# Row factors of the second norm taken in the output projection, and the second block's first rows turned during the first block's last up projection

## Chip, cores and metric

The kernel runs on one core of a Trainium2 chip. The metric is the device time in microseconds of one execution. Before the change the median of three runs is 1966.64 us (1966.62, 1966.64 and 1971.97).

## The reference, cut to what matters

Two independent sequences, a prompt of 512 rows and a sample of 1024 rows, each 1024 wide, go through one layer and a last norm. The change lies between the mixer and the SwiGLU.

```
def rmsnorm(x, g):
    y = x * rsqrt(mean(x * x, axis=-1) + EPS)
    return y * g

def trunk(x, ...):
    x = x + hybrid_mixer(rmsnorm(x, norm1_g), ..., w_out)   # mixed @ w_out
    x = x + swiglu(rmsnorm(x, norm2_g), w_gate, w_up, w_down)
    return rmsnorm(x, final_norm_g)

def swiglu(hn, w_gate, w_up, w_down):
    return (silu(hn @ w_gate) * (hn @ w_up)) @ w_down
```

## The kernel before

The 1536 rows are twelve tiles of 128 rows: a0 to a3 of the prompt, b0 to b7 of the sample. Until about 746 us the kernel computes the first norm, the mixer's projections, attention and the linear attention. Then comes the output projection: for each tile of the sample, class `Out` loads the mixed rows transposed (`mr`), splits them into a high and a low part (`mh`, `ml`), multiplies them with `w_out` in three column pieces (`acco` in PSUM), adds each piece to the residual row tile `xr` on VectorE (DVE), and `store` writes the finished tile to the DRAM tensor `x2d`.

The SwiGLU works on two blocks of six tiles: block 0 is a0 to a3, b0, b1; block 1 is b2 to b7. Each block goes through eleven groups of inner columns. A group has seven gate products and seven up products (a Strassen-like scheme over the operands b11, t2, b21, t3, t1, t4, b22, each as a high and a low part, into `gu` banks) and then six `down` steps, one for each row tile, of twelve matmuls each (two column halves of six, into `dn` banks, each half added to the accumulator `xa` on DVE). Weights are loaded by DMA (`rw_gate`, `rw_up`), combined on DVE with temporaries from the pool `sm`, and split into `cw_gate`, `cw_up` by ScalarE (ACT) and DVE.

The operands of a block are made by two methods. `rows(i)` loads row tile i of the block from `x2d` into `hx` (a pool of two buffers), squares it on ACT with a row sum (written to a `junk` tile of `sm`), makes the row factor (`ms` on DVE, a power on GpSimd), and scales `hx` by it and by the norm's weight on DVE. `turn(q)` takes row tiles 2q and 2q+1, transposes them on TensorE (PE) in four quarters of four 128x128 blocks (`trf`, sixteen in all), and makes the seven operands of these columns from them: copies and high parts on ACT, sums and low parts on DVE, with two temporaries `xt` from `sm`, which also has two buffers. So a block needs three turns, and the `hx` buffers of a turn are free for the next pair of rows when its transposes are done. For block 0 the turns stand in the output projection, between the tiles b2, b3 and b4, with two PSUM banks `tr`; for block 1 they stand at the boundary, in the last group of block 0, with the four `dn` banks.

The order of the program's lines is not the order on the engines: a scheduler orders the instructions of each engine, every engine runs its own in that order, and the DMAs named here are issued from one queue, SP's. At the boundary `rows(0)` and `rows(1)` of block 1 are written after up products 2 and 4 of the last group, and a turn after downs 0, 2 and 4, each followed by the rows of the next pair.

Of the kernel before, what the change touches and what calls it, by code (L numbers as in the profile page):

```python
# [8 lines left out]
F32 = mybir.dt.float32  # L9
F32R = mybir.dt.float32r  # L10
BF16 = mybir.dt.bfloat16
U32 = mybir.dt.uint32
AF = mybir.ActivationFunctionType
ALU = mybir.AluOpType
# [4 lines left out]
P = 128  # L19
D = 1024  # L20
KD = D // P
FF = 2816
NF = FF // P
EPS = 1e-6
# [19 lines left out]
def tile_trunk(ctx: ExitStack, tc: tile.TileContext, a: dict):  # L44
    nc = tc.nc
    seqs = [
        Seq("a", 512, 0, a["x_prompt"], a["y_prompt"], a["c_rope_a"], a["c_mask_a"]),
        Seq("b", 1024, ROT, a["x_sample"], a["y_sample"], a["c_rope_b"], a["c_mask_b"]),
    ]
# [3 lines left out]
    cst = ctx.enter_context(tc.tile_pool(name="cst", bufs=1))  # L53
    ident = cst.tile([P, P], F32, name="ident")
    nhalf = cst.tile([P, 2], F32, name="nhalf")
    nc.vector.memset(nhalf, -0.5)

    def rms_rstd(pool, ss, n, width, nm):

        ms = pool.tile([P, n], F32, tag="ms", name=f"ms_{nm}")  # L60
        nc.vector.tensor_scalar(out=ms, in0=ss, scalar1=1.0 / width, scalar2=EPS, op0=ALU.mult, op1=ALU.add)
        rs = pool.tile([P, n], F32, tag="rs", name=f"rs_{nm}")
        nc.gpsimd.tensor_tensor(out=rs, in0=ms, in1=nhalf[:, 0:n], op=ALU.pow)
        return rs

    def split(h, l, src):

        nc.scalar.copy(out=h, in_=src)  # L68
        nc.vector.tensor_tensor(out=l, in0=src, in1=h.bitcast(F32), op=ALU.subtract)  # L69
# [33 lines left out]
    def pool(stack, name, bufs, **kw):  # L103
        return stack.enter_context(tc.tile_pool(name=name, bufs=bufs, reuse_waits="tile", **kw))

    if True:
        w_p = pool(left, "w", 16, side="left")
        u_p = pool(left, "u", 12, side="left")
        t_p = pool(left, "tp", 3, side="left")
# [338 lines left out]
        class Gla:  # L448
# [250 lines left out]
            def store(self, j):  # L699
                s, g = self.s, self.g  # L700
                sg, sx = self.o.pop(j)
                tr = sc_p.tile([P, 2, P], F32, tag="sc", name="tro")
                for h in range(2):
                    nc.tensor.transpose(tr[:, h], sg[:, h * P:(h + 1) * P], ident)
                ot = sx.rearrange("p (k c) -> p k c", k=2)
                nc.scalar.copy(out=ot, in_=tr)
                for p0, t0, n in s.rows(j):
                    nc.sync.dma_start(
                        out=mixd[self.si][4 + 2 * g:6 + 2 * g, :, t0:t0 + n].rearrange("k p c -> p k c"),
                        in_=ot[:, :, p0:p0 + n],  # L710
                    )
# [23 lines left out]
        class Out:  # L735
# [8 lines left out]
            def load(self):  # L744
                j = self.j
                self.h = self.tile([P, KD, P], F32R, "mh")
                self.l = self.tile([P, KD, P], F32R, "ml")
                mix = mixd[self.si][:, :, j * P:(j + 1) * P].rearrange("k p c -> p k c")
                raw = self.tile([P, KD, P], F32, "mr")
                nc.sync.dma_start(out=raw, in_=mix)  # L750
                split(self.h, self.l, raw)
                self.x = self.tile([P, D], F32, "xr")
                nc.sync.dma_start(out=self.x, in_=self.s.x[0, j * P:(j + 1) * P, :])
# [6 lines left out]
                nc.vector.tensor_tensor(out=x, in0=ps, in1=x, op=ALU.add)  # L760

            def store(self):
                nc.sync.dma_start(out=x2d[self.si][self.j * P:(self.j + 1) * P, :], in_=self.x)


        def constants():
# [67 lines left out]
        for si, s in enumerate(seqs):  # L834
# [3 lines left out]
            n = 6 if si == 0 else 0  # L838
# [11 lines left out]
            last = at[3].core_steps()  # L850
# [21 lines left out]
    if True:  # L872
# [3 lines left out]
        tf_p = pool(right, "tf", 3, side="right")  # L876
        sm_p = pool(right, "sm", 2, side="right")
        g2 = cf.tile([P, D], F32, name="g2")
# [3 lines left out]
        NT = 6  # L882
# [4 lines left out]
        class Block:  # L887
# [10 lines left out]
            def rows(self, i):  # L898
                si, j = self.bt[i]
                hx = hx_p.tile([P, D], F32, tag="hx", name="hx")  # L900
                nc.sync.dma_start(out=hx, in_=x2d[si][j * P:(j + 1) * P, :])
                ss = tf_p.tile([P, 1], F32, tag="ss", name="ss")
                junk = sm_p.tile([P, D], BF16, tag="sm", name="junk")
                nc.scalar.activation(out=junk, in_=hx, func=AF.Square, accum_out=ss)
                rs = rms_rstd(tf_p, ss, 1, D, f"n2{self.blk}{i}")
                nc.vector.scalar_tensor_tensor(out=hx, in0=hx, scalar=rs, in1=g2, op0=ALU.mult, op1=ALU.mult)
                self.hx[i] = hx

            def residual(self):
# [39 lines left out]
        blocks = [Block(0)]  # L949
        outs = [lead] + [Out(1, j, u_p, "u") for j in range(1, sb.T)]  # L950
        outs[1].load()
        for j in range(sb.T):
# [6 lines left out]
            q = j - 2  # L959
# [18 lines left out]
        dn_p = pool(banks, "dn", 4, space=PSUM)  # L978
        NG = NF // 2
# [162 lines left out]
        AHEAD = 4  # L1142
# [23 lines left out]
        def group(key):  # L1166
            if key not in groups:
                groups[key] = Group(*key)
            return groups[key]

        def fetch(key, wn):
            if (*key, wn) not in fresh:
                fresh[*key, wn] = True
                raw(*key, wn)

        def prepare_to(m):
            nonlocal ready
            while ready < min(m, len(made)):
                _, key, wn, n = made[ready]
                if key[0] == 1 and len(blocks) < 2:  # L1180
                    blocks.append(Block(1))
                fetch(key, wn)
                group(key).w[wn].prepare(n)
                if wn == "w_up" and n == 0:
                    fetch(key, "w_down")
                ready += 1
# [4 lines left out]
        done = 0  # L1191
        for u in units:
            if u[0] == "p":
                _, key, wn, n = u
                last = key == (0, NG - 1)
                ahead = AHEAD
                prepare_to(done + ahead)
                if key == (1, 0) and wn == "w_gate" and n == 0:
                    blocks[1].residual()
                group(key).product(wn, n)  # L1200
                done += 1
                if wn == "w_up" and n in (3, 5):
                    group(key).load_down((n - 3) // 2)
                if last and wn == "w_up" and n in (2, 4):
                    nb = blocks[1] if len(blocks) > 1 else Block(1)
                    if len(blocks) < 2:
                        blocks.append(nb)
                    nb.rows((n - 2) // 2)
            else:
                _, key, i = u  # L1210
                group(key).down(i)
                if key == (0, NG - 1) and i % 2 == 0:
                    q = i // 2
                    nb = blocks[1]
                    nb.turn(q, dn_p, "dn")
                    if q + 1 < NP:
                        nb.rows(2 * q + 2)
                        nb.rows(2 * q + 3)
# [64 lines left out]
```

## Time and profile before

| | |
|---|---|
| median of the runs | 1966.64 us |
| profiled execution | 1971.83 us, its span 1970.1 us |
| PE busy | 1919.5 us (97%) |
| DVE, ACT, POOL busy | 1374.9 (70%), 847.7 (43%), 81.3 us (4%) |
| mean granted TensorE clock | 0.987 of full speed |
| output projection, last `acco` matmul | 923.99 us |
| block 0, first gate product | 927.72 us |
| boundary, from the last up product's end to block 1's first gate product | 1414.39 to 1458.02 us |

All times but the median are of the profiled execution, in us from its span's start. What lies around its span is 1.7 us; it took 5.2 us longer than the median. The engines' shares are of the span. PE is busy almost all the time, so time is lost where PE waits.

### The profile page before, as it was taken

Reading aid. Unit: us, or ns where it says so; the run is one execution under the profiler, and the core shown is the slowest. Engines: PE = TensorE matmul, PEld = TensorE weight load, DVE = VectorE, ACT = ScalarE, POOL = GpSimd, SP = SyncE. Lnnn points to the kernel's source line nnn. Section 1 sums busy time; section 2 is a strip of 40 time slices with the busy share of each in tenths; the row PEclk is TensorE's granted clock in tenths of the full one; section 3 lists DMA queues with packets and bytes.
Section 4 is the critical chain, followed back from the end, with each engine's and each line's share of the span. In section 5 each row is a group of like instructions: output and inputs, shape, how many; then the busy total and the mean of one; then the engine's idle time right before and its main releaser. Section 6 shows DMA issues by size and latency. Waiting matters only on the chain.

```text
span 1970.1 us, 31961 instructions
## 1 busy us (share of the span) xinstructions
PE 1919.5 (97%) x12212; PEld 1769.0 (90%) x12212; DVE 1374.9 (70%) x3158; ACT 847.7 (43%) x2018; POOL 81.3 (4%) x113
## 2 busy tenths in 40 slices
PE   7999999999999999999999999999979999999997
PEld 7888889899998888998999999999869999999996
DVE  5687765647576777564777777777787777777775
ACT  6665556645445455332433333333463333333333
POOL 1110001111000000000000000000020000000001
PEclk9999999999998999999999999999989999999999
DMA  5232230202302332455322222222242221222221
GB/s 145 58 93 82 61 99 23 66 4 56 99 25 71 92 99 79 145 187 186 114 65 65 73 92 71 65 65 80 70 171 88 84 65 65 68 83 65 65 65 65
DMA packets 149450, 163.14 MB, mean 83 GB/s; under 512 B 15856, under 2 KB 127536, under 8 KB 149296
## 3 DMA queue, kind: packets, MB, share of 16 engines
q1 hardware_dynamic: 149296, 161.09, 26.2%
q8 instruction: 96, 1.57, 0.3%
q14 instruction: 58, 0.48, 0.1%
HBM read 140.02 MB, written 21.04 MB: 82 GB/s over the span
## 4 chain that ended last, share of the span: by engine, by line
PE 89%; DVE 4%; DMA 2%; ACT 2%; issue 1%; POOL 1%; SPq 0%; POOLq 0%; DVEq 0%; ACTq 0%
PE gu L1042 32%; PE acc L82 7%; PE acc L84 6%; PE acc L83 6%; PE dn L84 6%; PE dn L82 6%; PE dn L83 6%; PE sc L300 4%; PE pv L400 3%; PE trp L377 2%; PE acco L82 2%; PE acco L83 2%; PE acco L84 2%; PE kv L641 2%; DMA rw_gate<-w_gate 1%
## 5 line engine op out<-in xcount | busy, mean ns | idle before, releaser
L1109 DVE TENSOR_TENSOR xa<-dn,xa 128x512 f32<-128x512 f32 x264 | 181.8, 691 | 146.3 <-PE dn L84 146.3
L82 PE MATMUL dn<-wd,g 128*128 128x512 f32 x528 | 206.7, 392 | 1.3 <-DVE xa L1109 1.0
L84 PE MATMUL dn<-wd,g 128*128 128x512 f32 x528 | 205.9, 390 | 0.2 <-DVE g L69 0.2
L83 PE MATMUL dn<-wd,g 128*128 128x512 f32 x528 | 205.8, 390 | 0.0
L68 ACT CAST wd<-rd 128x1024 fp32r<-128x1024 f32 x44 | 44.0, 1046 | 290.3 <-PE dn L84 289.9
L82 PEld LDWEIGHTS dn<-wd,g 128*128 128x128 f32 x528 | 99.5, 188 | 23.1 <-DVE xa L1109 2.2
L84 PEld LDWEIGHTS dn<-wd,g 128*128 128x128 f32 x528 | 99.2, 188 | 21.4 <-DVE g L69 0.6
L83 PEld LDWEIGHTS dn<-wd,g 128*128 128x128 f32 x528 | 99.3, 188 | 19.5
L1047 DVE TENSOR_TENSOR u<-gu,u 128x384 f32<-128x384 f32 x176 | 97.3, 553 | 25.6 <-PE gu L1042 25.4
L68 ACT CAST cw_gate<-rw_gate 128x512 fp32r<-128x512 f32 x110 | 66.1, 620 | 110.4 <-DMA rw_gate<-w_gate 53.3
L356 ACT ACTIVATE sm<-sm,st 128x256 f32<-128x256 f32 (+1 forms) x160 | 86.7, 543 | 58.7 <-DVE st L350 58.5
L82 PE MATMUL acc<-w_atb,hnh_b 128*128 128x384 f32 x256 | 91.7, 358 | 0.0
L68 ACT CAST cw_up<-rw_up 128x512 fp32r<-128x512 f32 x110 | 68.2, 621 | 51.2 <-PE gu L1042 49.5
L84 PE MATMUL acc<-w_atb,hnl_b 128*128 128x384 f32 x256 | 88.8, 347 | 0.0
L83 PE MATMUL acc<-w_atb,hnh_b 128*128 128x384 f32 x256 | 88.6, 346 | 0.0
L69 DVE TENSOR_TENSOR cw_up<-rw_up,cw_up 128x512 fp32r<-128x512 f32 x110 | 75.5, 688 | 7.9 <-ACT cw_up L68 7.2
L69 DVE TENSOR_TENSOR cw_gate<-rw_gate,cw_gate 128x512 fp32r<-128x512 f32 x110 | 75.2, 685 | 0.1
L377 PE MATMUL trp<-ident,sm 128*128 128x128 f32 x384 | 62.4, 288 | 0.8 <-ACT ptt L382 0.3
L345 DVE CUSTOM_DVE_ANT_0 sm<-sc,mask_b 128x256 f32<-128x256 f32 x128 | 50.1, 419 | 17.4 <-PE trqk L252 8.8
L82 PE MATMUL acco<-wo,mh_b 128*128 128x384 f32 (+1 forms) x192 | 61.5, 320 | 0.1
L83 PE MATMUL acco<-wo,mh_b 128*128 128x384 f32 (+1 forms) x192 | 61.2, 319 | 0.0
L84 PE MATMUL acco<-wo,ml_b 128*128 128x384 f32 (+1 forms) x192 | 61.2, 319 | 0.0
(410 smaller groups left out, 5744.0 us busy)
## 6 DMA issues: line engine op xcount, KB each, us to landing
rw_gate<-w_gate SPq DMA_DIRECT2D x22, 1024.0 KB, 5.4
rw_up<-w_up SPq DMA_DIRECT2D x22, 1024.0 KB, 7.5
rd<-w_down SPq DMA_DIRECT2D x22, 1024.0 KB, 4.9
wr_ata<-w_in SPq DMA_DIRECT2D x32, 192.0 KB, 2.5
wr_atb<-w_in SPq DMA_DIRECT2D x32, 192.0 KB, 2.6
wt<-lsed SPq DMA_DIRECT2D x32, 128.0 KB, 3.1
mr_b<-mixd_b SPq DMA_DIRECT2D x8, 512.0 KB, 4.7
xr_b<-x_sample SPq DMA_DIRECT2D x8, 512.0 KB, 4.4
```

The costliest lines, as they stand in the source:

```text
L68: nc.scalar.copy(out=h, in_=src)
L69: nc.vector.tensor_tensor(out=l, in0=src, in1=h.bitcast(F32), op=ALU.subtract)
L82: nc.tensor.matmul(out, xh, wh, start=(k == 0), stop=False)
L83: nc.tensor.matmul(out, xh, wl, start=False, stop=False)
L84: nc.tensor.matmul(out, xl, wh, start=False, stop=(k == n - 1))
L300: nc.tensor.matmul(outs[hd], lhs(x[b:b + 64]), rhs(y[b:b + 64]), start=(n == 0), stop=(n == 2))
L356: nc.scalar.activation(out=sm[:, cs], in_=sm[:, cs], func=AF.Exp, scale=0.125, bias=st[:, NM, pat, hd, i0 + g:i0 + g + 1], accum_out=st[:, ...
L377: nc.tensor.transpose(tr[:, i], sm[:, i * P:(i + 1) * P], ident)
L400: nc.tensor.matmul(self.pv[b:b + 64, i * P:(i + 1) * P], v, ptt[hd][:, n], start=(first and n == 0), stop=(last and n == 3),)
L1042: nc.tensor.matmul(ps, wc[:, wp, k], src[:, k], start=(own == n and k == 0 and i == 0), stop=(k == KH - 1 and i == 2), skip_group_check=True)
L1047: add = lambda o, i0: nc.vector.tensor_tensor(out=o, in0=ps, in1=i0, op=ALU.add)
L1109: nc.vector.tensor_tensor(out=acc[i][:, cs], in0=ps, in1=acc[i][:, cs], op=ALU.add)
```

## The change

The row factors of all twelve tiles are made where the tiles are finished: `Out.store` squares `xr` on ACT (into the `mr` tile, which is held until then), and `ms` and the power follow as before, into twelve small tiles `rs2` that live to the end. `rows` then is a load and a scaling. In the last up projection of block 0, `rows(0)` and `rows(1)` of block 1 are written after up product 0, and `turn(0)` with `rows(2)` and `rows(3)` after up product 6, ahead of the downs; `turn(1)` with the rows 4 and 5 follows down 0, and `turn(2)` follows down 2.

```diff
             def store(self):
                 nc.sync.dma_start(out=x2d[self.si][self.j * P:(self.j + 1) * P, :], in_=self.x)
+                ss = t_p.tile([P, 2], F32, tag="ss", name="ss")
+                nc.scalar.activation(out=self.raw.rearrange("p k c -> p (k c)"), in_=self.x, func=AF.Square,
+                                     accum_out=ss[:, 0:1])
+                ms = t_p.tile([P, 1], F32, tag="ms", name="ms_n2")
+                nc.vector.tensor_scalar(out=ms, in0=ss[:, 0:1], scalar1=1.0 / D, scalar2=EPS, op0=ALU.mult, op1=ALU.add)
+                rs = rs2[self.j + (seqs[0].T if self.si else 0)]
+                nc.gpsimd.tensor_tensor(out=rs, in0=ms, in1=nhalf[:, 0:1], op=ALU.pow)
...
             def rows(self, i):
...
-                ss = tf_p.tile([P, 1], F32, tag="ss", name="ss")
-                junk = sm_p.tile([P, D], BF16, tag="sm", name="junk")
-                nc.scalar.activation(out=junk, in_=hx, func=AF.Square, accum_out=ss)
-                rs = rms_rstd(tf_p, ss, 1, D, f"n2{self.blk}{i}")
-                nc.vector.scalar_tensor_tensor(out=hx, in0=hx, scalar=rs, in1=g2, op0=ALU.mult, op1=ALU.mult)
+                nc.vector.scalar_tensor_tensor(out=hx, in0=hx, scalar=rs2[self.blk * NT + i], in1=g2, op0=ALU.mult,
+                                               op1=ALU.mult)
...
-                if last and wn == "w_up" and n in (2, 4):
-                    nb = blocks[1] if len(blocks) > 1 else Block(1)
-                    if len(blocks) < 2:
-                        blocks.append(nb)
-                    nb.rows((n - 2) // 2)
+                if last and wn == "w_up":
+                    if n == 0:
+                        if len(blocks) < 2:
+                            blocks.append(Block(1))
+                        blocks[1].rows(0)
+                        blocks[1].rows(1)
+                    if n == 6:
+                        blocks[1].turn(0, dn_p, "dn")
+                        blocks[1].rows(2)
+                        blocks[1].rows(3)
             else:
                 _, key, i = u
                 group(key).down(i)
-                if key == (0, NG - 1) and i % 2 == 0:
-                    q = i // 2
+                if key == (0, NG - 1) and i in (0, 2):
+                    q = i // 2 + 1
                     nb = blocks[1]
                     nb.turn(q, dn_p, "dn")
```

What the engines run is seen at three places. The first is PE in the output projection, around block 0's first two turns (`trf` are transposes, `acco` the products). Before, the last four transposes of turn 0 and the first eight of turn 1 had this around them, with 67 `acco` matmuls between them (of two tiles):

```order
L82 MATMUL acco<-wo_9486,mh_b_10719 128x384
L923 MATMUL trf<-ident,hx 128x128 x4
L83 MATMUL acco<-wo_9486,mh_b_10719 128x384
...
L83 MATMUL acco<-wo_9466,mh_b_10887 128x384
L923 MATMUL trf<-ident,hx 128x128 x8
L84 MATMUL acco<-wo_9466,ml_b_10888 128x384
```

After the change 32 stand between them, all of the same tile:

```order
L83 MATMUL acco<-wo_9531,mh_b_10761 128x384
L929 MATMUL trf<-ident,hx 128x128 x4
L84 MATMUL acco<-wo_9531,mh_b_10761 128x384
...
L85 MATMUL acco<-wo_9982,ml_b_10762 128x384
L929 MATMUL trf<-ident,hx 128x128 x8
L83 MATMUL acco<-wo_10036,mh_b_10761 128x256
```

Turn 1 has moved ahead by half of the products; from turn 1's last transposes to turn 2's first there are 48 after the change.

The second is DVE at the same place after the change (`rs_2` and `rs_3` are the factors of row tiles 2 and 3, which turn 1 needs; `t2l` to `t4l` and `xt` are work of turn 0):

```order
L911 SCALAR_TENSOR_TENSOR hx<-hx,rs_2_66,g_10645 128x1024
L70 TENSOR_TENSOR t2l_10650<-xt_10860,t2h_10649 128x4x128
L70 TENSOR_TENSOR b22l_10660<-trf,b22h_10659 128x4x128
L70 TENSOR_TENSOR t3l_10654<-xt_10859,t3h_10653 128x4x128
L936 TENSOR_TENSOR xt_10860<-trf,xt_10860 128x512
L911 SCALAR_TENSOR_TENSOR hx<-hx,rs_3_67,g_10645 128x1024
L70 TENSOR_TENSOR t4l_10658<-xt_10860,t4h_10657 128x4x128
L761 TENSOR_TENSOR xr_b_10767<-acco,xr_b_10767 128x384 x2
```

Before, `t2l` to `xt` stood ahead of the first scaling; now they stand between the two.

The third is the boundary. On PE sixteen `trf` now stand directly behind the last up product, ahead of the twelve matmuls of down 0; turn 1's sixteen stand behind these twelve, turn 2's behind the 24 of downs 1 and 2, and downs 3 to 5 are mixed with block 1's first gate products. Before, the order was twelve, turn 0, 24, turn 1, 24, turn 2, twelve, gate. On DVE, after the change, this follows the last up product (`rs_8` and `rs_9` belong to row tiles 2 and 3 of block 1):

```order
L70 TENSOR_TENSOR b11l_15400<-trf,b11h_15399 128x4x128
L70 TENSOR_TENSOR b21l_15404<-trf,b21h_15403 128x4x128
L70 TENSOR_TENSOR g_10_15396<-u_15167,g_10_15396 128x384
L70 TENSOR_TENSOR cw_gate_15890<-s1w_gate_15498,cw_gate_15890 128x512
L70 TENSOR_TENSOR cw_gate_15907<-rw_gate_15476,cw_gate_15907 128x512
L911 SCALAR_TENSOR_TENSOR hx<-hx,rs_8_72,g_10645 128x1024
L1010 TENSOR_TENSOR rw_gate_15476<-rw_gate_15476,s2w_gate_15499 128x4x128
L911 SCALAR_TENSOR_TENSOR hx<-hx,rs_9_73,g_10645 128x1024
L936 TENSOR_TENSOR xt_15545<-xt_15544,trf 128x512
L1115 TENSOR_TENSOR xa_11479<-dn,xa_11479 128x512
```

The scalings of the second pair have moved ahead of `xt<-xt,trf`, the last reader of one of turn 0's four PSUM banks, and ahead of the first `xa`; before, both pieces of `xa` of down 0 and all of turn 0's operations but one stood ahead of them. The third pair's scalings likewise stand ahead of turn 1's two `xt<-trf,xt`.

## Rows read from the trace of the kernel before

**Rows 1.** Page, part 1: busy time, share and instructions of each engine.

```profile
PE 1919.5 (97%) x12212; PEld 1769.0 (90%) x12212; DVE 1374.9 (70%) x3158; ACT 847.7 (43%) x2018; POOL 81.3 (4%) x113
```

**Rows 2.** PE's waits, whole run: us in total, times, longest.

```profile
PE trf L923 <- DVE hx L906: 16.1, 4, 8.4
PE gu L1042 <- ACT cw_gate L68: 3.5, 1, 3.5
```

**Rows 3.** PE's waits in the output projection, 850 to 930 us.

```profile
PE trf L923 <- DVE hx L906: 1.7, 2, 1.2
```

**Rows 4.** PE's waits at the boundary, 1414 to 1460 us.

```profile
PE trf L923 <- DVE hx L906: 14.4, 2, 8.4
```

**Rows 5.** PE at the boundary: start, us, instruction [idle before, releaser].

```profile
1414.39 0.39 PE L82 MATMUL dn<-wd,g 128*128 128x512 f32 x1
...
1417.69 1.98 PE L923 MATMUL trf<-ident,hx 128*128 128x128 f32 x16
...
1422.02 0.50 PE L82 MATMUL dn<-wd,g 128*128 128x512 f32 x1 [0.97 <-DVE xa L1109]
...
1434.84 3.68 PE L923 MATMUL trf<-ident,hx 128*128 128x128 f32 x16 [8.35 <-DVE hx L906]
...
1450.64 3.65 PE L923 MATMUL trf<-ident,hx 128*128 128x128 f32 x16 [6.07 <-DVE hx L906]
...
1458.02 0.34 PE L1042 MATMUL gu<-b11h,cw_gate 128*128 128x384 f32 x1
```

**Rows 6.** Stretches: length, busy of PE, PEld, DVE, ACT, POOL, clock, DMA.

```profile
890.00:893.00 3.00, 3.00 (x22) 2.74 (x22) 2.49 (x4) 1.07 (x2) 0.00 (x0) 1.00 0.66 207
...
926.50:933.20 6.70, 5.48 (x17) 5.26 (x18) 5.68 (x9) 3.80 (x7) 0.00 (x0) 0.50 1.06 393
...
1431.60:1438.40 6.80, 3.56 (x17) 3.56 (x18) 5.93 (x11) 3.10 (x6) 5.34 (x5) 0.50 0.14 58
...
1448.70:1455.50 6.80, 4.86 (x19) 4.45 (x20) 3.96 (x8) 3.39 (x6) 5.65 (x7) 0.50 0.20 78
```

**Rows 7.** PE in the output projection, around block 0's turns.

```profile
863.17 0.61 PE L923 MATMUL trf<-ident,hx 128*128 128x128 f32 x4
...
874.78 1.06 PE L923 MATMUL trf<-ident,hx 128*128 128x128 f32 x8 [0.50 <-DVE hx L906]
...
889.90 1.06 PE L923 MATMUL trf<-ident,hx 128*128 128x128 f32 x8 [1.23 <-DVE hx L906]
...
927.72 0.69 PE L1042 MATMUL gu<-b11h,cw_gate 128*128 128x384 f32 x1 [3.45 <-ACT cw_gate L68]
```

**Rows 8.** SP's queue, DMA issues of the next pair of rows.

```profile
862.07 2.08 SPq L901 DMA_DIRECT2D hx<-x2d_a  x2
...
1419.19 1.71 SPq L901 DMA_DIRECT2D hx<-x2d_b  x2
```

**Rows 9.** Tile hx, its DMAs, 840 to 930 us.

```profile
DMA to landing us min/median/max: 3.5/5.3/5.9
```

**Rows 10.** Tile hx, its DMAs, 1380 to 1460 us.

```profile
DMA to landing us min/median/max: 4.2/4.6/5.0
```

**Rows 11.** DVE at the boundary.

```profile
1416.98 0.69 DVE L69 TENSOR_TENSOR cw_gate<-s1w_gate,cw_gate 128x512 fp32r<-128x512 f32 x1
...
1422.67 0.69 DVE L930 TENSOR_TENSOR xt<-xt,trf 128x512 f32<-128x512 f32 x1
...
1430.83 1.28 DVE L906 SCALAR_TENSOR_TENSOR hx<-hx,rs_n,g 128x1024 f32<-128x1024 f32 x1 [0.66 <-POOL rs_n L63]
```

**Rows 12.** ACT at the boundary.

```profile
1418.37 0.59 ACT L933 COPY xt<-trf 128x512 f32<-128x512 f32 x1 [0.75 <-PE trf L923]
...
1428.76 1.06 ACT L904 ACTIVATE junk<-hx 128x1024 bf16<-128x1024 f32 x1 [0.67 <-DVE t3l L69]
```

**Rows 13.** DVE in the output projection, second scaling for turn 1.

```profile
873.35 1.28 DVE L906 SCALAR_TENSOR_TENSOR hx<-hx,rs_n,g 128x1024 f32<-128x1024 f32 x1 [0.27 <-POOL rs_n L63]
```

**Rows 14.** ACT in the output projection.

```profile
890.62 0.59 ACT L933 COPY xt<-trf 128x512 f32<-128x512 f32 x1 [3.46 <-PE trf L923]
```

More of the change, by code (lines that the diff above doesn't have):

```diff
@@ L55, in tile_trunk @@
     nhalf = cst.tile([P, 2], F32, name="nhalf")
+    rs2 = [cst.tile([P, 1], F32, name=f"rs2_{i}") for i in range(sum(s.T for s in seqs))]
     nc.vector.memset(nhalf, -0.5)
@@ L748, in load @@
                 mix = mixd[self.si][:, :, j * P:(j + 1) * P].rearrange("k p c -> p k c")
-                raw = self.tile([P, KD, P], F32, "mr")
+                raw = self.raw = self.tile([P, KD, P], F32, "mr")
                 nc.sync.dma_start(out=raw, in_=mix)
@@ L1195, in tile_trunk @@
                 last = key == (0, NG - 1)
-                ahead = AHEAD
-                prepare_to(done + ahead)
+                prepare_to(done + AHEAD)
                 if key == (1, 0) and wn == "w_gate" and n == 0:
```

## The prediction

> **What bounds the kernel now.** The page comes first: PE is busy for 97% of the span, DVE for 70%, ACT for 43% [rows 1]. So an edit is worth what it does to PE's waits. The list of PE's waits over the whole run shows few: the longest sum is transposes (`trf`) that wait for a scaled row tile `hx`, 16.1 us in four times, then 3.5 us for the first gate weights of block 0 [rows 2]. By window, 14.4 us of the 16.1 lie at the boundary of the blocks, in two waits, and 1.7 us in the output projection, in two others [rows 3, 4]. The timeline of PE at the boundary shows them: turn 0 goes through without a wait, turn 1 waits 8.35 us, turn 2 6.07 us; down 1 waits 0.97 us for an `xa` [rows 5]. From 1414.39 to 1458.02 are 43.63 us. Behind each long wait sixteen transposes took 3.68 and 3.65 us where turn 0's took 1.98.
>
> The windows say why: from 1431.6 to 1438.4 and from 1448.7 to 1455.5 the granted clock is 0.50, the lower of the two levels, each time behind one of these waits; so it is from 926.5 to 933.2, behind a single wait of 3.45 us in a dense stage, while a wait of 1.23 us left it at 1.00 [rows 5 to 7]. So the boundary's two waits cost 14.4 us and 1.7 us each for slow transposes, about 18 us. That is what the change can win at most there.
>
> Why does turn 1 wait? The next pair's loads can be issued only when turn 0's transposes give the `hx` buffers back (SP issues at 1419.19, 1.5 us behind the start of turn 0) [rows 5, 8]. They land in 4.6 us [rows 10]; then the Square waits for a buffer of `sm`, which `t3l` frees, at 1428.76 [rows 12]; the first scaling stands at 1430.83 [rows 11]. From the issue to the scaling are 11.6 us, of which the load is 4.6.
>
> **The change, part by part: factors.** Six Squares, `ms` and powers go from block 0's rows and six from block 1's; twelve come into `store`. ACT sits idle 3.46 us between tiles in the output projection [rows 14], and a Square is 1.06 us [rows 12], so eight Squares of the sample's tiles cost nothing there while ACT keeps that room (8.5 us if it had none, all on ACT). The four of the prompt's tiles lie among attention's work, ahead of 850 us, and of PE's two largest waits the one for ACT, 3.5 us, is that of the gate weights [rows 2]; I take 0, bounds -1 and +2. The `mr` tile is held longer by one Square: 0.
>
> **The boundary.** Count from T = 1414.39, the end of the last up product. Turn 0's transposes now end at T+2.0. Down 0 comes next and needs a PSUM bank of the four that turn 0 fills. The first to come free is that of the ACT copy `xt` (0.59 us), which needs a buffer of `sm`; these hold the weights' temporaries until the last `cw_gate` splits. Before, the split from `s1w_gate` ended at 1417.67, T+3.3 [rows 11]. Now `b11l` and `b21l` (0.69 each, as the `xt` row) stand ahead: T+4.7, and the copy ends at T+5.3 to T+5.9, by one further split. So a wait of 3.3 to 3.9 us; I take 3.7. Six matmuls (half of the 3.3 us of a down) later, at T+7.3, the second half needs the bank that `xt<-xt,trf` frees. On DVE the two `hx` scalings stand ahead of it. Their loads are issued at T+1.8 and land at T+6.4; then 1.28, one 0.69, 1.28, and `xt` 0.69: T+10.3. A wait of 3.0; with landings of 4.2 and 5.0, 2.6 and 3.4. Turn 1's four quarters need banks that `xa`, `xt` and copies free one after the other, 0.6 to 0.7 each, behind the same queue: I take three waits of 1, bounds 0.5 and 1.5 each. The third pair is issued when turn 1's transposes end, E; landing at E+4.8, then two scalings and six operations of about 0.65 (through `t3l`) end at E+11.2, while PE has 18 matmuls and small waits, some 5 to 7 us: a wait of 4 to 6, I take 4. Small waits at turn 2 and between gate and downs, by the 0.97 of before [rows 5]: 2, bounds 0 and 3. Sum 3.7 + 3.0 + 3.0 + 4 + 2 = 15.7, against 15.4 before (14.4 + 0.97). The wait has been cut up, not removed. What is left to gain: the transposes of the turn that now runs ahead of the waits are at full clock (1.7), and part of PE's short gaps at 0.50 before. I take -2.5, bounds -8 (waits at their low ends) and +1.5 (clock low behind three waits instead of two).
>
> At this place a rule speaks against the change. The row: 3.45 us of waiting was enough for a clock of 0.50 over the next 6.7 us [rows 6, 7]. The Trainium skill, TensorE: Matmul & The Clock Gate, "HAM oscillation — how this bites in real kernels", says that a wait for data in every tile makes the engine pay the transition each time anew. By that rule three waits of 3 to 4 us would cost three slow stretches where two stood; the boundary would then give -0.8 instead of -2.5 and the sum would be about 1972. The trace agrees as far as the one row of 3.45 us goes.
>
> **The output projection.** Here the order shows a cost that the diff doesn't. Turn 1's first transposes stood 67 products behind turn 0's last; now 32. PE took 11.1 us from 863.17 to where it began to wait (874.78 - 0.50 = 874.28) [rows 7]: (11.1 - 0.6)/67 = 0.16 us a product, so 32 take 5.0 to 5.6 (these are all of the wider form), and PE is there at L+5.9, with L = 863.17 as start of turn 0's last transposes. What it needs is the second scaling. Both loads still wait for these transposes: SP's issue of the pair ends at 862.07 + 2.08 = L+1.0 [rows 8], the second begins 0.35 earlier, and lands 5.3 later: L+6.0 [rows 9]. On DVE the first scaling holds back `t2l` to `xt`, which stand between the two: 1.28 + 4 x 0.6 + 1.28 = 5.0, L+11.0. Before it ended at 873.35 + 1.28 = L+11.5 [rows 13]: the Square and the power were hidden behind turn 0's splits, so leaving them out saves half a microsecond only. The wait becomes 11.0 - 5.9 = 5.1 instead of 0.5; with landings of 3.5 and 5.9, 3.3 to 5.7. So +4.6, bounds +2.8 and +5.2. Turn 2 stands 48 products behind, 8 us, against 6.0 + 2.5 for two scalings in a row: about the 1.23 of before, 0 (-1.2 to +0.8). PE is dense here, so nothing behind takes it back: the gate weights' load behind the last products moves along. Nearly 5 us of waiting should bring the clock down as 3.45 did: 6.7 us at half speed with 5.48 busy lose 2.7 [rows 6]; since the stretch can be shorter, I take 2 (0 to 3.4). Together +6.6.
>
> **Sum.** 6.6 - 2.5 = +4 on the profiled 1971.83: 1976. That execution was 5.2 us above the median of 1966.64, and the sum goes by differences: 1966.6 + 4 = 1970.6. A measurement of this kernel tells 0.3%, 5.9 us, from no change, so this is "same", near the slow edge.
>
> **Rivals.** Slower: the clock decides. Output projection at its upper ends (5.2 + 0.8 + 3.4 = 9.4) and a boundary that gives nothing, since the three waits each bring the 0.50: 1976. For it: [rows 6]. Against it: slow stretches overlap waits that DVE and DMA set. It decides as soon as the loss in the output projection exceeds the boundary's gain by 5.9. Faster: the boundary's later waits shrink, because DVE isn't as late as I count (the Squares are gone from ACT, so the splits run sooner): only the 3.7 and the small 2 remain, 15.4 + 3.4 - 5.7 = -13, with the output projection at +2.8 and no slow stretch: -10, 1956.5. For it: 11.6 us from issue to scaling become some 6. Against it: `xt` stands behind the scalings. The Trainium skill, DMA: Bandwidth & Descriptors, "Rules for kernel authors", advises to issue a load early and wait for it late; by it the early pair would make this rival true, but only that pair is early. That the change doesn't do what it says is excluded by the order.
>
> **Numbers.** Forecast 0.50, slower rival 0.32, faster rival 0.18. The forecast ends within 0.3% of before, the two rivals beyond it, so the chances of same, slower and faster are these three. The forecast's own range is 1964 to 1973; 8 in 10 need the slow case to 1977 and the fast one to 1960.
>
> **What would show it.** Right: PE waits about 5 us at turn 1 in the output projection, with a clock of 0.50 behind; at the boundary no wait above 5, four or more of 1 to 4, summing to 13 to 18. Wrong: waits at the boundary that sum to under 8, or no `trf` wait above 2 us ahead of 900.

## The result and the profile after

The changed kernel took 1985.61 us (median of 6 runs, 1979.66 to 1989.65), the kernel before 1971.18 us beside it (6 runs, 1966.62 to 1974.03): a ratio of 1.0075 with an interval of 1.0054 to 1.0096. It is slower by 14.4 us. The forecast was 4 us more than before and the slower rival 9.4, so the measured change lies beyond both. (In absolute times, 1970.6 and a range up to 1977 were given; 4.5 us of the distance to 1985.61 come from the kernel before, whose median is 1971.18 here and was 1966.64 when the prediction was made.)

The profiled execution took 1986.15 us, its span 1984.4 against 1970.1; the mean granted clock is 0.987 in both. The first part of the page after, which answers to [rows 1]:

```profile
PE 1936.2 (98%) x12212; PEld 1784.4 (90%) x12212; DVE 1381.6 (70%) x3158; ACT 848.6 (43%) x2018; POOL 79.6 (4%) x113
```

This line says that the prediction, which counted waits and clock, looked in the wrong place. PE has as many matmuls as before, at the same mean clock, and is idle for less time: 1984.4 - 1936.2 = 48.2 us against 1970.1 - 1919.5 = 50.6. It is its busy time that has grown, by 16.7 us.

PE's waits after, over the whole run (in total, times, longest), beside [rows 2]:

```profile
PE trn L163 <- DMA wr_vag<-w_in: 8.2, 1, 8.2
PE trf L929 <- DVE hx L911: 4.8, 2, 3.8
PE dn L83 <- ACT xt L939: 3.5, 1, 3.5
PE gu L1048 <- ACT cw_gate L69: 3.4, 1, 3.4
PE dn L83 <- DVE xa L1115: 3.2, 2, 2.8
...
PE gu L1048 <- DVE u L1053: 2.2, 1, 2.2
PE dn L83 <- DVE xt L936: 1.6, 3, 0.7
```

(The first line, a wait near the kernel's start, was 8.0 us before and isn't in [rows 2].) The two long waits of the boundary [rows 4] are gone. `trf` waits for `hx` only in the output projection now, where PE's timeline, beside [rows 7], has:

```profile
866.49 0.61 PE L929 MATMUL trf<-ident,hx 128*128 128x128 f32 x4
...
876.48 1.76 PE L929 MATMUL trf<-ident,hx 128*128 128x128 f32 x8 [3.80 <-DVE hx L911]
...
892.22 0.74 PE L929 MATMUL trf<-ident,hx 128*128 128x128 f32 x5 [1.04 <-DVE hx L911]
...
934.51 0.53 PE L1048 MATMUL gu<-b11h,cw_gate 128*128 128x384 f32 x1 [3.39 <-ACT cw_gate L69]
```

Turn 1 waits 3.80 us instead of 0.50, and its eight transposes take 1.76 us instead of 1.06; block 0 begins 934.51 - 927.72 = 6.8 us later. Not all of this arose there. Block 0's first transposes, ahead of these waits, stand here, before and after:

```profile
859.93 1.04 PE L923 MATMUL trf<-ident,hx 128*128 128x128 f32 x8
...
862.26 1.03 PE L929 MATMUL trf<-ident,hx 128*128 128x128 f32 x8
```

Behind both, PE has the same 360 `acco` matmuls to do before block 0. So 2.3 us of the 6.8 were there already, and 4.5 were lost behind. The 2.3 say little: in seven other kernels below that differ from the one before only in places of tiles or at the boundary (e1, e3 to e7, e9), this start lies between 857.60 and 863.34 us.

At the boundary, beside [rows 5], PE shows:

```profile
1425.36 1.91 PE L929 MATMUL trf<-ident,hx 128*128 128x128 f32 x16
1430.78 0.79 PE L83 MATMUL dn<-wd,g 128*128 128x512 f32 x1 [3.51 <-ACT xt L939]
...
1434.40 0.77 PE L83 MATMUL dn<-wd,g 128*128 128x512 f32 x1 [0.69 <-DVE xt L936]
...
1437.10 2.10 PE L929 MATMUL trf<-ident,hx 128*128 128x128 f32 x8
1439.37 0.87 PE L929 MATMUL trf<-ident,hx 128*128 128x128 f32 x4 [0.17 <-DVE b22l L70]
1440.49 0.66 PE L929 MATMUL trf<-ident,hx 128*128 128x128 f32 x4 [0.25 <-ACT xt L939]
...
1449.06 0.50 PE L83 MATMUL dn<-wd,g 128*128 128x512 f32 x1 [2.84 <-DVE xa L1115]
```

The wait is cut up, as forecast. The granted clock of these stretches (columns as in [rows 6]):

```profile
876.80:880.20 3.40, 3.40 (x18) 3.40 (x17) 2.36 (x5) 1.17 (x2) 0.00 (x0) 0.51 0.02 5
...
1429.80:1440.00 10.20, 8.36 (x24) 5.89 (x24) 9.70 (x15) 5.03 (x11) 0.00 (x0) 0.51 0.10 42
1450.00:1453.40 3.40, 3.40 (x16) 2.83 (x15) 3.04 (x7) 1.54 (x5) 0.55 (x1) 0.52 0.00 0
1477.50:1480.90 3.40, 3.40 (x11) 3.40 (x12) 2.73 (x5) 2.07 (x4) 0.00 (x0) 0.51 1.01 333
```

Behind the waits of 3.80, 3.51, 2.84 and 2.2 us the granted clock was close to 0.50, the lower of its two levels; the second `dn` wait, 0.69 us, lies within the 10.20 us.

**Where the time went.** Take a stretch in which PE waits for nothing: the last up product of block 0, 84 matmuls with `cw_up` as stationary operand and `b11` to `b22` as moving ones. Before, its first matmul starts thus (PE's timeline), and what stands behind the 84 starts at 1414.39 [rows 5]; the second row is block 1's first up product:

```profile
1399.83 0.34 PE L1042 MATMUL gu<-b11h,cw_up 128*128 128x384 f32 x1
...
1473.26 0.34 PE L1042 MATMUL gu<-b11h,cw_up 128*128 128x384 f32 x1
```

After:

```profile
1410.52 0.34 PE L1048 MATMUL gu<-b11h,cw_up 128*128 128x384 f32 x1
...
1483.27 0.34 PE L1048 MATMUL gu<-b11h,cw_up 128*128 128x384 f32 x1
```

With 1425.36 as its end, the product takes 14.84 us instead of 14.56: 176.7 ns from matmul to matmul instead of 173.3. The window of this product, before:

```profile
1399.90:1414.30 14.40, 14.40 (x85) 14.40 (x84) 11.06 (x18) 6.18 (x11) 0.00 (x0) 1.00 0.46 146
```

and after:

```profile
1410.60:1425.20 14.60, 14.60 (x85) 14.60 (x84) 11.23 (x18) 6.28 (x11) 0.00 (x0) 1.00 0.47 144
```

PE is busy throughout, the clock is 1.00, and DMA, DVE and ACT do the same work beside it in both.

The groups by shape, 960 to 1360 us (busy, mean ns of one), show which matmuls are longer, before:

```profile
L82 PE MATMUL dn<-wd,g 128*128 128x512 f32 x216 | 84.0, 389 | 0.0
...
L1042 PE MATMUL gu<-t2h,cw_up 128*128 128x384 f32 x72 | 19.8, 336 | 0.0
```

and after:

```profile
L83 PE MATMUL dn<-wd,g 128*128 128x512 f32 x210 | 81.7, 389 | 0.0
...
L1048 PE MATMUL gu<-t2h,cw_up 128*128 128x384 f32 x64 | 17.8, 338 | 0.0
```

The down products are the same, the gate and up products are not. There are 44 of these (2 blocks x 11 groups x 2). The first gate product of each block is disturbed by waits and low clock, and after the change block 1's is mixed with downs, so these two are left out. The other 42, each taken from its first matmul to what stands behind its last, sum to 612.3 us before and 622.2 after: 9.9 of the 14.3 us by which the span has grown. Along the timeline the 14.3 are made up of 2.3 us ahead of block 0's first transposes, 4.5 from there to block 0's first gate product, 4.2 from there to the end of its last up product, -1.0 from there to block 1's first up product, and 4.3 behind that.

The change touches none of these matmuls. What it touches is where their operands lie. The twelve `rs2` tiles are made among the constants, each takes 32 bytes of every partition in the built program, and every tile on that side of SBUF that is placed behind them moves by 384 bytes: the stationary `cw` tiles begin at byte 33824 instead of 33440. The moving tiles are placed from the other side and stay, the first at 143328. Counted modulo 256, the moving operand lies 64 bytes ahead of the stationary one before, and 192 after. The down products have both operands (`wd`, `g`) on the side that moved, so they lie to each other as before, and their pace is as before. The theory is that this place, and not the schedule, makes the gate and up products slower. The rival is that the schedule does it: the new order and the factors' instructions, by their waits and by what they make the other engines do beside PE.

### The profile page after: what moved, and what is told of

It is laid out like the page before. It is cut to its first block, busy times and chain, and to the rows that moved or that the text cites. A ratio compares the mean times of both kernels' runs of the same rounds, so it can differ in the third digit from the quotient of the medians.

```text
span 1984.4 us, 31961 instructions
## 1 busy us (share of the span) xinstructions
PE 1936.2 (98%) x12212; PEld 1784.4 (90%) x12212; DVE 1381.6 (70%) x3158; ACT 848.6 (43%) x2018; POOL 79.6 (4%) x113
## 4 chain that ended last, share of the span: by engine, by line
PE 88%; DVE 4%; DMA 3%; issue 1%; ACT 1%; POOL 1%; SPq 1%; DVEq 0%; POOLq 0%; ACTq 0%
PE gu L1048 32%; PE acc L83 7%; PE acc L85 6%; PE acc L84 6%; PE dn L83 6%; PE dn L85 6%; PE dn L84 6%; PE sc L301 4%; PE pv L401 3%; PE trp L378 2%; PE acco L83 2%; PE acco L84 2%; PE acco L85 2%; PE kv L642 2%; DMA rw_gate<-w_gate 1%
```

## Experiments

**The tiles alone.** Kernel e1 is the kernel before with twelve tiles that nothing uses:

```diff
     nhalf = cst.tile([P, 2], F32, name="nhalf")
+    pad = [cst.tile([P, 1], F32, name=f"pad_{i}") for i in range(12)]
```

> The kernel before with twelve unused 128x1 tiles in the pool of constants, which move every tile allocated behind them on that side of SBUF by 384 bytes (as the twelve factor tiles of the change do) and leave every engine's order as it was. Theory A (the move of addresses slows the gate and up matmuls): their pitch goes from 173.3 to about 176.3 ns, 3696 of them take about 11 us longer, and the time rises by 9 to 12 us. Theory B (the slower pitch comes from the changed order of work, or is a state of the run): the pitch stays 173.3 ns and the time stays within 3 us of before.

It took 1982.75 us against 1969.93, a ratio of 1.0055 (1.0034 to 1.0076), with the `hx` waits of before: the first row of the list of PE's waits of e1, whole run, has the same 16.1 us as [rows 2].

```profile
PE trf L924 <- DVE hx L907: 16.1, 4, 8.4
```

Its last up product, in PE's timeline, from the first matmul to the first `dn`:

```profile
1405.37 0.34 PE L1043 MATMUL gu<-b11h,cw_up 128*128 128x384 f32 x1
...
1420.21 0.39 PE L83 MATMUL dn<-wd,g 128*128 128x512 f32 x1
```

14.84 us, as in the changed kernel, with not one instruction of the change. Its 42 products sum to 623.0.

**The change without the shift of place.** e2 is the changed kernel with four more tiles, so that the shift is 512 bytes and the distance 64 again:

```diff
     rs2 = [cst.tile([P, 1], F32, name=f"rs2_{i}") for i in range(sum(s.T for s in seqs))]
+    pad = [cst.tile([P, 1], F32, name=f"pad_{i}") for i in range(4)]
```

> The changed kernel with four more unused 128x1 tiles, so that the tiles behind them stand 512 instead of 384 bytes off their place of before; the order on all engines is that of the changed kernel. Theory A with an effect that repeats every 512 bytes or less: the pitch of gate and up matmuls returns to 173.3 ns, the time falls by about 11 us against the changed kernel and stands 2 to 6 us above the kernel before, which is what the waits alone make. Theory A with another period: a pitch between 173 and 178 ns. Theory B: the pitch stays at 176.3 ns and the time at 12 to 16 us above before.

It took 1976.02 us against 1969.93, 1.0028 (1.0016 to 1.0040): what the schedule itself costs, some 5.5 us. Its 42 products sum to 612.1. The schedule falls as the main cause. Its waits at the boundary, 1400 to 1480 us, are these:

```profile
PE dn L84 <- ACT xt L940: 3.6, 1, 3.6
PE dn L84 <- DVE xa L1116: 3.0, 2, 2.7
PE gu L1049 <- DVE u L1054: 2.2, 1, 2.2
PE dn L84 <- DVE xt L937: 2.2, 2, 2.0
```

**Other shifts.** e3 and e4 are e1 with 8 and 4 tiles (256 and 128 bytes), one execution each.

> The kernel before with eight unused 128x1 tiles, a shift of 256 bytes. Theory A: if the effect repeats every 256 bytes the pitch of gate and up matmuls is 173.3 ns and the time that of before; if every 512, another pitch, with 3 us more for each 0.8 ns. Theory B: 173.3 ns.

> The kernel before with four unused 128x1 tiles, a shift of 128 bytes. Theory A: if the effect repeats every 256 bytes, this equals the shift of 384, about 176.3 ns and 9 to 12 us longer; if every 512 bytes, something else between. Theory B: 173.3 ns and no change.

e3 took 1974.86 and e4 1983.88 us, against 1969.93. Their last up products took 14.56 and 14.84 us. Of the four shifts, 256 and 512 leave the product as it was, and 128 and 384 lengthen it alike: as far as these four go, the shift modulo 256 counts, not the number of tiles. The time of e3 is a miss: "that of before" was expected, and it lies above the highest of the thirteen runs of before (1974.71), with the products at their old pace (612.9 us for the 42). Its first `acco` matmul already stands at 750.30 us where before had 746.45; one execution doesn't say more.

**Which side?** In e5 only the weights are shifted by 128 bytes, in e6 only the moving operands, in e7 both. A second tile behind the pool keeps what follows in its place modulo 256:

```diff
+        padc = pool(right, "padc", 1, side="right").tile([P, 32], F32, name="padc_t")
         hb_p = pool(right, "hb", 1, side="right")
+        padd = pool(right, "padd", 1, side="right").tile([P, 32], F32, name="padd_t")
...
         wr_p = pool(left, "wr", 2, side="left")
+        pada = pool(left, "pada", 1, side="left").tile([P, 32], F32, name="pada_t")
         wc_p = pool(left, "wc", 6, side="left")
+        padb = pool(left, "padb", 1, side="left").tile([P, 32], F32, name="padb_t")
```

(e5 has the lower two, e6 the upper two, e7 all but `padd`, so in e7 the tiles behind the moving ones are off by 128, too.)

> The kernel before, with 128 bytes of unused space ahead of the six weight tiles (cw, the stationary operand of gate and up matmuls) and 128 behind them, so that only these stand at another place within 256 bytes; the moving operands (b11 to b22), the order and all else stay. If the place of the stationary operand alone decides: 176.3 ns pitch and some 11 us longer. If the moving operand's place alone decides: 173.3 ns, no change. If other tiles that moved (raw weights, down weights, accumulators) decide: 173.3 ns.

> The kernel before, with 128 bytes ahead of the moving operands (b11 to b22) and 128 behind, so that only these stand at another place within 256 bytes. If the stationary operand's place alone decides: 173.3 ns, no change. If the distance of the two decides: 176.3 ns, some 11 us longer.

> The kernel before with both the weight tiles and the moving operands 128 bytes off (in opposite directions, which is the same within 256). If the distance of the two decides: 173.3 ns, no change. If the stationary operand's place alone decides: 176.3 ns, some 11 us longer.

One execution each, beside 1971.24 us: 1974.68, 1980.57 and 1969.33. The rows of e6, where only the moving operands moved:

```profile
1403.84 0.34 PE L1044 MATMUL gu<-b11h,cw_up 128*128 128x384 f32 x1
...
1418.68 0.39 PE L82 MATMUL dn<-wd,g 128*128 128x512 f32 x1
```

and of e7, where both did:

```profile
1397.93 0.34 PE L1045 MATMUL gu<-b11h,cw_up 128*128 128x384 f32 x1
...
1412.50 0.39 PE L82 MATMUL dn<-wd,g 128*128 128x512 f32 x1
```

14.84 and 14.57 us. Moving either operand alone slows the product, moving both does not: the distance of the two decides whether it is slow. It does not alone decide how slow. e5 took 14.67 us, which none of the expectations had. Its rows, with those of e4 behind them:

```profile
1399.94 0.34 PE L1044 MATMUL gu<-b11h,cw_up 128*128 128x384 f32 x1
...
1414.61 0.39 PE L82 MATMUL dn<-wd,g 128*128 128x512 f32 x1
...
1405.77 0.34 PE L1043 MATMUL gu<-b11h,cw_up 128*128 128x384 f32 x1
...
1420.61 0.39 PE L83 MATMUL dn<-wd,g 128*128 128x512 f32 x1
```

In the built programs of e4 and e5 every one of the 3696 gate and up matmuls has its operands and its output at the very same addresses (`cw` from 33568, the moving ones from 143328). What differs is where other tiles lie: `rw_gate`, `rw_up` and the tiles ahead of them are 128 bytes off their old places in e4 and not off in e5; `wd`, `g`, `xa` and their neighbours are 128 off in e4 and 256 in e5. So these other places, or something that follows from them, have a part in the pace. Which, was not tried.

**The change taken apart.** e8 is e2 with the old order at the boundary (the factors alone); e9 is the kernel before with the new order there (the early turn alone).

> The changed kernel with the old order at the boundary (rows after up products 2 and 4, turns after downs 0, 2 and 4), so only the factors are made in the output projection; padded to a shift of 512 bytes. If the factors' part makes the loss in the output projection (rows without a Square let the scheduler put turn 1's transposes 32 products behind turn 0's): one wait of some 3.8 us there as in the changed kernel, block 0 starts 4 to 5 us later than before; at the boundary the two waits for hx shrink by about 2 us each, since the Square and the power are gone. In all 0 to 5 us above before. If the turn that was moved ahead made that loss: no wait above 1.5 us in the output projection, and a time 2 to 5 us below before.

> The kernel before with the new order at the boundary alone (rows 0 and 1 after up product 0, turn 0 and rows 2 and 3 after up product 6, turns after downs 0 and 2); rows keep their own Squares, no factors in the output projection, no address moves. If turn 0 ahead of the downs costs rather than gains (it takes down 0's banks while DVE is still at the weights): the output projection is that of before, with waits of 0.5 and 1.2 us; the boundary takes 2 to 5 us longer than before, with a wait of down 0 for an xt of 3 to 4 us; the time is 2 to 5 us above before. If it gains as the change means it to: the boundary is at least 4 us shorter and the time 3 to 8 us below before.

e8 took 1971.96 us against 1971.24, 1.0003 (0.9991 to 1.0015); e9 1974.43 against 1970.82, 1.0022 (1.0011 to 1.0032). In e8, PE's waits from 850 to 1480 us:

```profile
PE dn L84 <- DVE b22l L71: 5.9, 1, 5.9
PE trf L930 <- DVE hx L912: 4.2, 2, 3.7
...
PE dn L84 <- DVE xa L1116: 2.4, 3, 1.1
PE dn L84 <- DVE xt L937: 1.3, 2, 1.0
```

Both `hx` waits of e8 (4.2 us) lie in the output projection. From block 0's first transposes (863.83) to its first gate product (935.34) PE took 71.5 us, 3.7 more than before. So the factors alone make the longer wait there, and alone they also take both long `hx` waits away at the boundary, for one of 5.9 us at a down (they were expected to shrink by 2 us each). In e9, at 1414 to 1460 us:

```profile
PE trf L923 <- DVE hx L906: 14.7, 2, 8.6
PE dn L82 <- ACT xt L933: 3.8, 2, 3.6
```

The early turn alone keeps the 14.4 us of [rows 4] and adds a wait at the downs. From the last up product's end to block 1's first up product PE took 58.9 us before (1414.39 to 1473.26), 53.8 in e8 (1422.28 to 1476.03), 64.2 in e9 (1415.63 to 1479.85), 56.5 in e2 (1418.34 to 1474.83) and 57.9 in the changed kernel (1425.36 to 1483.27). There the factors alone win 5.1 us, the early turn alone loses 5.3, and the two together (e2) win 2.4: with the factors, the early turn takes back 2.7 of the 5.1.

The parts add up: 0.55% (e1) + 0.03% (e8) + 0.22% (e9) = 0.80%, measured 0.75%.

**Can the rest be had?** e10 is e8 with the rows of each pair asked for in the other order, to shorten the wait in the output projection (the cut shows one of four such swaps; the others are those of block 0's first pair and of block 1):

```diff
-                    blocks[0].rows(2 * q + 2)
                     blocks[0].rows(2 * q + 3)
+                    blocks[0].rows(2 * q + 2)
```

> The factors alone, at a shift of 512 bytes, with the two row tiles of each pair asked for in the other order: a turn's first four transposes need the second tile of its pair, and its buffer is the first to come free. If the wait for hx in the output projection is the chain of the second load and the second scaling: the wait of 3.7 us becomes two of about 2 us, block 0 starts 2 us earlier than with the factors alone, and the time is 0 to 4 us below before. If the wait is set by the splits on DVE: no change against the factors alone, within 2 us of before.

It took 1970.04 us against 1970.82, 0.9993 (0.9983 to 1.0003). The waits at 850 to 930 us:

```profile
PE trf L930 <- DVE hx L912: 1.8, 1, 1.8
PE trf L930 <- DVE b22l L71: 1.4, 1, 1.4
```

3.2 us instead of 4.2, in two parts of which only one is a wait for `hx`. Against e8, from block 0's first transposes to its first gate product took 70.2 us instead of 71.5; the gain is not told from none.

**Two last questions of place**, one execution each beside 1970.82 us: e11 is the changed kernel with the moving operands shifted by 128 bytes (distance 64 again, by `padc` alone), e12 the kernel before with two tiles (64 bytes, distance 0).

> The changed kernel as it is (weights 384 bytes off), with 128 bytes of unused space ahead of the moving operands, so that the distance of the two within 256 bytes is that of before; the order is that of the changed kernel. If the distance decides: a pitch of 173.3 to 173.6 ns and a time of 1970 to 1980 us. If the weights' place itself or that of the tiles around them decides: 176.3 ns and 1980 to 1990 us.

> The kernel before with two unused tiles, a shift of 64 bytes, so that weights and moving operands stand at the same place within 256 bytes (before 64 apart, in the changed kernel 192). If the pitch follows the distance with a minimum around 64: between 173.3 and 176.3 ns. If any distance but 64 is slow: 176 ns or more. If only 192 is slow: 173.3 ns.

e11's products are at 14.56 us, and the 42 sum to 612.1, as expected; its time, 1980.15, stands at the upper edge of what was expected. Block 0 starts 4.5 us later in it than in e2 (936.88 against 932.40), 3.7 of it ahead of block 0's first transposes, and its time lies within the spread of e2's own ten runs (1971.88 to 1980.40), so one execution does not tell the two apart. e12 took 1979.95 us, and not through these products (612.7 for the 42): its first `acco` matmul stands at 754.02 us where before had 746.45 (743.28 to 750.30 in the seven others with the same instructions up to there). So 7.6 us are lost ahead of it, where the `acc` matmuls of 256 columns follow each other at 119.6 ns in the mean instead of 115.5 (from their start times; 115.3 to 117.0 in the others). Which operands of theirs lie worse was not taken apart.

## Why the prediction was wrong, by its own steps

**The step that failed** stands in the part on factors, "I take 0", and with it in the sum, "6.6 - 2.5 = +4". That part counted the twelve factors as instructions of ACT, DVE and GpSimd, and never as twelve tiles that take a place. They move the weights, and that costs 9.9 us in 42 of the gate and up products (e1, with nothing but the tiles, 10.7; its median is 0.55%, some 11 us, above before). Behind the term stands the premise that "an edit is worth what it does to PE's waits": here PE waited less and worked more slowly. Neither rival had this mechanism; forecast and rivals all argued over waits and clock.

Without it the sum of +4 was of the right size: e2 measures the schedule alone at 5.5 us (3.2 to 7.9). Its terms were not all right, and part of the agreement is luck. In e2's profiled execution, one of the two fastest of the ten (1972.81), 4.6 us are lost from block 0's first transposes to its first gate product and 2.4 are won at the boundary, 2.2 in all; where the rest of the median's 5.5 lies, that trace doesn't show.

A reading was wrong, too: the second largest of PE's waits is not the one for ACT's gate weights (3.5 us) but one of 8.0 us of a transpose (`trn`) for the DMA of `wr_vag`. It is 8.2 us after the change, so nothing came of it.

**Output projection, +6.6.** Block 0 starts 6.8 us later (4.7 in e2, 7.6 in e8), but that this is nearly the 6.6 is luck: 2.3 us lie ahead of block 0's first transposes. From there on the loss is 4.5 (4.6 in e2, 3.7 in e8). Turn 1's wait was to grow by 4.6 with bounds of 2.8 and 5.2, and grew by 3.3. PE arrived as counted (876.48 - 3.80 = L+6.2, counted L+5.9). The second scaling ended at L+9.85 where L+11.0 was counted. The clock behind it was to cost 2, and 3.40 us of busy time at 0.51 lose 1.7. The term was sized 2.1 too high, 1.3 of it in turn 1's wait.

**Boundary, -2.5.** The prediction's waits sum to 0.3 more than before and its clock gives 1.7 back; for the other 1.1 of the -2.5 it names short gaps and no figure. In e2 the stretch from the last up product's end to block 1's first up product is 2.4 us shorter, in the changed kernel 1.0 (1.2 at the old pace of the one gate product in it). The terms: the first down 3.7 counted, 3.51 measured; the second half 3.0 counted, 0.69 (2.0 in e2), since the six matmuls ahead of it ran at 0.50 and took 2.9 us where e2's took 1.65; turn 1's quarters 3.0 counted, 0.42 measured; the third pair's chain 4 counted, 2.84, at a down and not at the turn; the small ones 2 counted, and with the 2.2 of the first gates some 4 measured. They sum to 11.5, between the prediction's marks for right (13 to 18) and wrong (under 8). The rule of the Trainium skill, TensorE: Matmul & The Clock Gate, "HAM oscillation — how this bites in real kernels", that each wait for data is paid again in clock, agrees with the changed kernel: three stretches near 0.50 at the boundary where two stood, 10.20 + 3.40 + 3.40 = 17.0 us against 6.8 + 6.8 = 13.6. It does not agree with e2, whose waits are nearly the same: its clock was at 0.50 for 6.8 and 3.4 us only, and behind the last wait, 2.2 us that ended at 1470.56, it stayed at 1.00 (window as in [rows 6]):

```profile
1468.00:1472.00 4.00, 1.82 (x11) 1.50 (x10) 3.37 (x6) 0.26 (x1) 0.59 (x2) 1.00 0.99 362
```

So not each of these waits was paid again.

**Why the early turn gains nothing** was right in kind: the wait for `hx` becomes a wait for `xt` and `xa` behind the same DVE queue. What was not seen is that the factors alone would gain 5.1 us there (the "faster" rival's mechanism, in a part of the change), and that the early turn takes back 2.7 of them. **Factors hidden on ACT, 0**, is not contradicted as far as ACT's work goes: e8 as a whole is at +0.03%, with a loss of 3.7 us in the output projection and a gain of 5.1 at the boundary. A cost of some 2 us ahead of block 0's first transposes can't be excluded: they start at 860.00 to 863.83 us in the five kernels with factors, at 857.60 to 863.34 in the eight without (e12 left out).

## What to carry to other kernels

A small tile among the constants moves every tile behind it. When PE's busy time grows and its count of matmuls and its waits do not, take one dense product of before and after, compare the pitch, and then the operands' addresses, before looking for a reason in the schedule; a build that adds only the tiles separates the two. And of a change in two parts, time each part alone: at the boundary one wins 5 us here where the other loses 5, and over the whole run neither part is faster than before.

## What the runs showed of the hardware

| kernel | distance, bytes mod 256 | last up product, us | from matmul to matmul, ns | 42 products, us |
|---|---|---|---|---|
| before | 64 | 14.56 | 173.3 | 612.3 |
| e2, e3, e7, e11 | 64 | 14.56 to 14.57 | 173.3 to 173.5 | 612.1 to 612.9 |
| e12 | 0 | 14.59 | 173.7 | 612.7 |
| after, e1, e4 | 192 | 14.84 | 176.7 | 622.2 to 623.0 |
| e6 | 192 | 14.84 | 176.7 | 622.4 |
| e5 | 192 | 14.67 | 174.6 | 617.0 |

The distance is the start of the moving operand minus that of the stationary one, both from the built programs; the times are worked out from the start times in PE's timelines. These matmuls stream 384 columns of four bytes at a granted clock of 1.00, and PE waits for no semaphore in them: where two operands lie to each other changes their pace by up to 2%. The pace goes in levels, 14.56, 14.67 and 14.84 us for a product, and a kernel does not always keep to one. At a distance of 64 nearly all are at 14.56, and the few longer ones keep its pace but for single gaps; at 192 most are at 14.84, but in the changed kernel four are at 14.67 and one at 14.56, and in e5 36 are at 14.67, three at 14.84 and one at 14.56, at one and the same distance. The Trainium skill, SBUF — State Buffer, "SBUF: two separate sides", says that on the engines' side only one shared port pair causes contention and that PE never waits on anyone. It says nothing there of where PE's own operands lie to each other; in this case PE's pace differs by place alone, 173.3 and 176.7 ns. Whether PE waits for another engine's access in the slow products, against the page, no run here shows.

What inside PE or SBUF makes the difference was not shown: no run here looks below an instruction. Open too is which tiles beside the operands make e5 faster than e4, why single products leave their kernel's level, and by which operands e12 is slower ahead of its first `acco` matmul.
